# The S5 recurrence of a fp32 decoder layer in chunks of eight tokens

## The chip, the cores and the metric

The kernel runs on one core of a Trainium2 chip. Its engines are named as the profile names them: PE multiplies matrices (PEld loads its weights), DVE and ACT work elementwise, POOL fills and issues some DMAs, SP issues nearly all DMAs. SBUF holds tiles of 128 partitions, PSUM holds what PE writes. The metric is the device time of one execution in microseconds (us). A kernel's time is the median of its runs. Everything is computed in fp32 or in pairs of rounded fp32 halves ("hi" and "lo", type fp32r on PE).

## What is computed

One layer of a hybrid decoder: 512 prompt tokens and 8 sequences of 8 sample tokens (576 columns in all), width 2048. One wide projection of x feeds three mixers (S5, gated linear attention, a convolution), whose gated outputs are merged, projected, normalised. Only S5 concerns the change. It has 64 groups of 16 channels; each group has 64 complex states that decay on their own:

```python
def s5_mixer(u, h0_re, h0_im, a_re, a_im, log_dt, b_re, b_im, c_re, c_im, d):
    lam = lax.complex(a_re, a_im)
    dt = jnp.exp(log_dt)[:, None]
    a_bar = jnp.exp(lam * dt)
    b_bar = ((a_bar - 1.0) / lam)[..., None] * lax.complex(b_re, b_im)
    bu = jnp.einsum('btgc,gpc->btgp', ug, b_bar)
    bu = bu.at[:, 0].add(a_bar * h0)
    _, h = lax.associative_scan(combine, (a_seq, bu), axis=1)   # h[t] = a_bar * h[t-1] + bu[t]
    c = lax.complex(c_re, c_im)
    y = jnp.einsum('btgp,gcp->btgc', h, c).real + d * ug
    return y, h[:, -1].real, h[:, -1].imag
```

The prompt starts from a zero state, each sample sequence from its own given state h0. After it come GELU, a gated product, and a projection. The last states are outputs too.

## The kernel before

**The weight stream.** All dense products are jobs of `run_jobs`. A job makes 128 output channels for all 576 columns from a column block of a weight matrix. Its weights come in units of eight k-tiles (512 KB, line 313, three buffers `raw`), are split by ACT into `hi` (line 70 through `split` and `prep`) and by DVE into `lo` (line 77), and PE makes three products for each k-tile (hi by x hi, hi by x lo, lo by x hi), each in two pieces of 288 columns (line 347). So a k-tile is six products, half a unit 24, a unit 48, and a job with 16 k-tiles 96. Two PSUM accumulators `mm` take turns.

**Background work.** S5, attention and convolution are Python generators. Between two half units the emitter calls `pump`, which gives each running generator a credit worth some microseconds of DVE; a `yield` with a number spends credit, a bare `yield` waits for the next half unit. That fixes the order in which the program is written. A scheduler with a timeline then sets the order of each engine's queue; an instruction whose data it thinks late is moved behind others. Once set, each engine takes its queue in order.

**S5 before.** The jobs of the first part are eight blocks of u (128 channels, eight groups, four pairs of groups), each followed by five gate jobs. For each block `s5_block` splits u, copies the halves to pairs with 16 DMAs (line 596), loads B and C, turns both by 4 transposes, and spreads B with 16 DMAs (line 629). For each of the four pairs, `s5_front` makes B u for the real and imaginary part (4 products of 128x128 weights and 288 columns, fp32r, line 649) and a table of cosines and sines for all 576 columns; `s5_back` rotates, runs the real decay as a scan over all 512 tokens (line 696) and one over the samples (698), and rotates back. `s5_out` multiplies with C: 16 fp32 products on four column tiles of PE (line 726), adds d u, applies GELU and stores a tile `yd`, which `ys_load` reads back much later. Transposes stand under line 99, elementwise DVE operations under 77, 90, 92, 95, ACT under 70: these are helpers.

Of the kernel before, what the change touches and what calls it, by code (L numbers as in the profile page):

```python
# [8 lines left out]
F32 = mybir.dt.float32  # L9
# [31 lines left out]
class K:  # L41
# [9 lines left out]
    # ------------------------------------------------------------ helpers  # L51
# [125 lines left out]
    # ------------------------------------------------------------ constants  # L177
# [27 lines left out]
    def vectors(self):  # L205
        """Channel vectors, one column for each block of 128."""
# [3 lines left out]
        par = c([128, 1], I32, name="par")  # L210
        nc.vector.tensor_scalar(par, part, 4, 1, op0=OP.logical_shift_right, op1=OP.bitwise_and)
        self.par = c([128, 4], F32, name="parf")
        self.ts(self.par[:, 1:2], par, 1.0)
        self.ts(self.par[:, 0:1], par, -1.0, 1.0)
        self.ts(self.par[:, 2:4], self.par[:, 0:2], -1.0)
# [71 lines left out]
    # ------------------------------------------------------------ weight stream  # L287
# [3 lines left out]
    def run_jobs(self):  # L291
# [60 lines left out]
        # the first two jobs advance together, a block of x at a time  # L352
# [69 lines left out]
    # ------------------------------------------------------------ S5  # L422
    def s5_prep(self):
# [93 lines left out]
        # rotation tables, entries 0..63, for all pairs, eight pairs to a slot  # L517
# [5 lines left out]
        def double(m, tc_, ts_, j0, nj):  # L523
            n = 2 ** m
            cm = self.cos[:, m, j0:j0 + nj, None].to_broadcast([128, nj, n])
            sm = self.sin[:, m, j0:j0 + nj, None].to_broadcast([128, nj, n])
# [22 lines left out]
        # sample states: a_bar * h0 as [(g2 p), part, s, pair]  # L549
# [9 lines left out]
        self.ah0 = self.alloc()  # L559
        nc.gpsimd.memset(self.ah0[:, 512:], 1.0)  # L560
        nc.gpsimd.memset(self.ah0[:, 512:].rearrange("p (s e) -> p s e", s=8)[:, :, 0:1], 0.0)
        self.mk64 = self.ah0[:, 512:]
        ah = self.ah0[:, :512].rearrange("p (t s j) -> p t s j", t=2, s=8)
        hv = p.rearrange("p (t s j) -> p t s j", t=2, s=8)
        tm = h0[:, :256].rearrange("p (s j) -> p s j", s=8)
        ar, ai = abr[:, None, :].to_broadcast([128, 8, 32]), abi[:, None, :].to_broadcast([128, 8, 32])
        self.mul(ah[:, 0], hv[:, 0], ar)
        self.mul(tm, hv[:, 1], ai)
        self.sub(ah[:, 0], ah[:, 0], tm)
        self.mul(ah[:, 1], hv[:, 1], ar)  # L570
        self.mul(tm, hv[:, 0], ai)
        self.add(ah[:, 1], ah[:, 1], tm)
        self.free(h0)
        self.ST = self.alloc()
        self.done.add("s5prep")
        yield 2.0

    def s5_block(self, b, st):
        """Block b of four pairs: its operands."""
# [3 lines left out]
        u = self.u[b]  # L583
        uh, ul = self.split(u)
        w, e = self.alloc(), self.alloc()
        st["w", b] = w
        # C of this block, [(g2 p), (g8 c)] with the other group of each pair zero
        for pt, nm in enumerate(("s5_c_re", "s5_c_im")):
            nc.sync.dma_start(e[:, 256 + pt * 64:320 + pt * 64], i[nm][0, 8 * b:8 * b + 8].rearrange("g c p -> (g c) p"))
            for g in range(2):  # L590
                self.pin(self.act(e[:, pt * 128 + g * 64:pt * 128 + g * 64 + 64], e[:, 256 + pt * 64:320 + pt * 64],
                                  scale=self.par[:, 2 * pt + g:2 * pt + g + 1]))
        us = [self.alloc(F32R) for _ in range(4)]
# [3 lines left out]
        self.free(uh, ul)  # L597
        st["us", b] = us
        # B of this block, [(g2 p), pair, (g2' c)] with the other group of each pair zero
        z = self.alloc()  # L600
        nc.gpsimd.memset(z[:, 0:256], 0.0)
        for pt, nm in enumerate(("s5_b_re", "s5_b_im")):
            nc.sync.dma_start(z[:, 256 + 64 * pt:320 + 64 * pt].rearrange("q (j c) -> q j c", j=4),
                              i[nm][0, 8 * b:8 * b + 8].rearrange("(j g) p c -> (g p) j c", g=2))

# [3 lines left out]
        yield  # L609
        for pt, (x, y, op) in enumerate(((256, 320, OP.subtract), (320, 256, OP.add))):  # L610
            self.mul(v(384), v(x), fr)
            self.mul(v(448), v(y), fi)
            zz = z[:, pt * 128:(pt + 1) * 128].rearrange("q (j c) -> q j c", j=4)
            for g in range(2):
                q = slice(g * 64, g * 64 + 64)
                self.tt(zz[q, :, g * 16:g * 16 + 16], v(384)[q], v(448)[q], op)
        p = self.aux()
        for pt in range(2):
            self.tr(p[:, pt * 128:(pt + 1) * 128], z[:, pt * 128:(pt + 1) * 128])
            self.tr(p[:, 256 + pt * 128:384 + pt * 128], e[:, pt * 128:(pt + 1) * 128])  # L620
        yield 1.0
        bt = self.alloc(F32R)
        self.act(bt[:, 0:256], p[:, 0:256])
        self.act(w[:, 0:256], p[:, 256:512])
        self.sub(bt[:, 256:512], p[:, 0:256], bt[:, 0:256].bitcast(F32))
        lb = [self.alloc(F32R) for _ in range(2)]
        for d in range(4):
            for q in range(4):
                nc.sync.dma_start(lb[d // 2].bitcast(F32)[32 * q:32 * q + 32, (d % 2) * 256:(d % 2) * 256 + 256],
                                  bt.bitcast(F32)[32 * d:32 * d + 32, (q // 2) * 256:(q // 2) * 256 + 256])  # L630
        self.free(e, z, bt)
        st["lb", 2 * b], st["lb", 2 * b + 1] = lb
        yield 0.4
        for _ in range(BLK_WAIT):
            yield

    def s5_front(self, j, st):
        """Pair j of groups: B u and its rotation table."""
        nc = self.nc
        b, jj = divmod(j, 4)  # L640
        lb = st["lb", j // 2]
        # B u
        us = st["us", b][jj]
        bu = self.alloc(), self.alloc()
        for pt in range(2):
            o = (jj % 2) * 256 + pt * 128
            for h in range(2):
                p = self.aux()
                nc.tensor.matmul(p[:, :H], lb[:, o:o + 128], us[:, h * H:(h + 1) * H], start=True, stop=True)  # L649
                self.act(bu[pt][:, h * H:(h + 1) * H], p[:, :H])  # L650
            for _ in range(B_WAIT):
                yield
        # e^(i theta t)
        Ct, St, tmp = self.alloc(), self.alloc(), self.alloc()
        g, o = divmod(j, 8)
        for x, y in ((Ct, self.TC[g]), (St, self.TS[g])):
            self.act(x[:, 0:64], y[:, o * 64:(o + 1) * 64])
            self.act(x[:, 512:576].rearrange("p (s e) -> p s e", s=8), y[:, None, o * 64:o * 64 + 8].to_broadcast([128, 8, 8]))
        for m in range(6, 9):
            n = 2 ** m  # L660
            cm, sm = self.cos[:, m, j:j + 1], self.sin[:, m, j:j + 1]
            self.act(tmp[:, 0:n], St[:, 0:n], scale=sm)
            self.act(tmp[:, 256:256 + n], Ct[:, 0:n], scale=sm)
            self.stt(Ct[:, n:2 * n], Ct[:, 0:n], cm, tmp[:, 0:n], OP.mult, OP.subtract)
            self.stt(St[:, n:2 * n], St[:, 0:n], cm, tmp[:, 256:256 + n], OP.mult, OP.add)
            if m == 7:
                yield 0.7
        self.free(tmp)
        yield 0.7
        self.free(us)  # L670
        if jj % 2:
            self.free(lb)
        st["f", j] = (Ct, St, bu)

    def s5_back(self, j, st):
        """Pair j: rotation into the frame in which the decay is real, scan, rotation back."""
        nc = self.nc
# [1053 lines left out]
```

## Time and profile before

| what | value |
|---|---|
| median of 2 runs | 2398.74 us (2397.85 to 2399.63) |
| span of the profiled execution, first to last instruction | 2393.7 us |
| time of the profiled execution apart from its span | not recorded by itself; the median lies 5.0 us above the span |
| mean granted clock of PE over the span | 0.996 |
| S5 beside the stream | from about 60 to about 740 us |
| longest part of the chain by line | L347, 93% |

The page's second part cuts the span into 40 slices of 60 us. Each digit is the busy share of a slice in tenths:

```profile
PE   8999999999999999999999999999999999999998
PEld 7999999999999999999999999999999999999997
DVE  4889989989895443299998875344444553344556
ACT  4444544454445533332222233232232232232332
POOL 0000000000001010000000000000000000000000
PEclk9999999999999999999999999999999999999998
DMA  7444344444433343243333534344443323232223
```

S5 lies in slices 2 to 13, attention behind it up to slice 18, then the convolution. Two things help in reading on. A product's listed mean of some 295 ns is its length in the pipeline; the time from one start to the next is what a product costs PE. And an engine that is busy is not the one that sets the end unless others wait for it, which the chain (part 4 of the page) and the waits say.

### The profile page before, as it was taken

To read this page: it belongs to the slowest core of one execution; us is meant where nothing else is said; L and a number is where in the kernel's file an instruction comes from. 1 tells how busy PE (TensorE), PEld (TensorE's weight loads), DVE (VectorE), ACT (ScalarE), POOL (GpSimd) and SP (SyncE) were. 2 spreads that over 40 slices of the span, in tenths; PEclk is the share of its full clock that TensorE was granted. 3 is DMA by queue.
4 is the path that set the end of the run, shared out by engine and by line. 5 is a ranking of instruction groups with operands and counts; after the bars stand their busy time and mean duration, and the time that the engine had idled before them with its cause. 6 is when DMAs were issued, how large, how long until landed. Compare 5 with 4: busy or idle time off the path is not lost.

```text
span 2393.7 us, 44249 instructions
## 1 busy us (share of the span) xinstructions
PE 2378.1 (99%) x17908; PEld 2339.5 (98%) x17908; DVE 1549.4 (65%) x3084; ACT 861.0 (36%) x1802; POOL 33.3 (1%) x76
## 2 busy tenths in 40 slices
PE   8999999999999999999999999999999999999998
PEld 7999999999999999999999999999999999999997
DVE  4889989989895443299998875344444553344556
ACT  4444544454445533332222233232232232232332
POOL 0000000000001010000000000000000000000000
PEclk9999999999999999999999999999999999999998
DMA  7444344444433343243333534344443323232223
GB/s 204 120 120 133 106 138 128 122 118 124 132 96 91 104 126 111 81 147 108 94 85 105 155 96 144 86 128 118 123 116 112 110 80 88 80 96 82 80 76 101
DMA packets 424605, 267.13 MB, mean 112 GB/s; under 512 B 25673, under 2 KB 395917, under 8 KB 424385
## 3 DMA queue, kind: packets, MB, share of 16 engines
q1 hardware_dynamic: 421904, 256.87, 38.1%
q0 software_dynamic: 2496, 7.43, 0.9%
q8 instruction: 141, 2.31, 0.4%
q14 instruction: 64, 0.52, 0.1%
HBM read 219.22 MB, written 32.07 MB: 105 GB/s over the span
## 4 chain that ended last, share of the span: by engine, by line
PE 98%; DMA 1%; DVE 0%; SPq 0%; ACT 0%; issue 0%; DVEq 0%; ACTq 0%
PE mm L347 93%; PE aux L99 1%; PE two L99 1%; PE aux L649 1%; PE two L726 1%; DVE sl L95 0%; DMA sl<-in_x_sample 0%; PE two L963 0%; PE aux L962 0%; DMA sl<-in_w_in 0%; PE two L965 0%; DMA sl<-in_x_prompt 0%; PE two L1005 0%; PE two L814 0%; PE aux L940 0%; PE two L1001 0%
## 5 line engine op out<-in xcount | busy, mean ns | idle before, releaser
L347 PE MATMUL mm<-xh,hi 128*128 128x288 f32 (+1 forms) x4096 | 886.2, 298 | 2.4 <-ACT hi L70 1.9
L347 PE MATMUL mm<-xl,hi 128*128 128x288 f32 (+1 forms) x4096 | 886.8, 297 | 0.0
L347 PE MATMUL mm<-xh,lo 128*128 128x288 f32 (+1 forms) x4064 | 875.6, 296 | 0.0
L70 ACT ACTIVATE hi<-raw 128x512 fp32r<-128x512 f32 (+1 forms) x696 | 435.3, 626 | 1198.0 <-PE mm L347 1160.4
L77 DVE TENSOR_TENSOR lo<-raw,hi 128x512 fp32r<-128x512 f32 (+1 forms) x692 | 471.1, 681 | 571.4 <-ACT hi L70 534.5
L347 PEld LDWEIGHTS mm<-xh,hi 128*128 128x128 f32 x4096 | 659.1, 189 | 8.9 <-issue 2.8
L347 PEld LDWEIGHTS mm<-xl,hi 128*128 128x128 f32 x4096 | 661.0, 189 | 2.9 <-issue 1.2
L347 PEld LDWEIGHTS mm<-xh,lo 128*128 128x128 f32 x4064 | 655.4, 189 | 1.0 <-issue 0.4
L77 DVE TENSOR_TENSOR sl<-sl,sl 128x576 f32<-128x576 f32 (+9 forms) x842 | 502.8, 625 | 57.0 <-ACT sl L70 48.2
L347 PE MATMUL mm<-sl,hi 128*128 128x288 f32 x2944 | 510.3, 295 | 0.0
L347 PEld LDWEIGHTS mm<-sl,hi 128*128 128x128 f32 x2944 | 432.2, 188 | 0.5 <-ACT sl L70 0.2
L347 PE MATMUL mm<-sl,lo 128*128 128x288 f32 x1472 | 314.3, 295 | 0.0
L347 PEld LDWEIGHTS mm<-sl,lo 128*128 128x128 f32 x1472 | 236.7, 188 | 0.0
L95 DVE SCALAR_TENSOR_TENSOR sl<-sl,cw,sl 128x64 f32<-128x64 f32 (+1 forms) x480 | 216.3, 512 | 0.0
L70 ACT ACTIVATE sl<-sl 128x64 f32<-128x64 f32 (+5 forms) x293 | 107.8, 403 | 95.8 <-DVE sl L77 42.0
L70 ACT ACTIVATE sl<-sl,sl 128x128 f32<-128x128 f32 (+2 forms) x192 | 70.7, 411 | 37.8 <-DVE sl L95 27.3
L77 DVE TENSOR_TENSOR sl<-mm,sl 128x576 f32<-128x576 f32 x48 | 36.3, 756 | 70.9 <-PE mm L347 70.9
L70 ACT ACTIVATE sl<-mm,bias 128x576 f32<-128x576 f32 x112 | 81.2, 725 | 0.1
L696 DVE TENSOR_TENSOR_SCAN sl<-s5r,sl 128x512 f32<-128x512 f32 x64 | 77.9, 1217 | 0.0
L70 ACT ACTIVATE sl<-aux 128x288 f32<-128x288 f32 (+8 forms) x221 | 72.8, 371 | 11.1 <-PE aux L962 3.4
L95 DVE SCALAR_TENSOR_TENSOR sl<-sl,sl,sl 128x128 f32<-128x128 f32 (+2 forms) x192 | 64.3, 365 | 4.4 <-ACT sl L70 4.2
L70 ACT ACTIVATE sl<-two 128x128 f32<-128x128 f32 (+6 forms) x58 | 20.1, 352 | 65.8 <-DVE sl L1451 34.5
(181 smaller groups left out, 800.6 us busy)
## 6 DMA issues: line engine op xcount, KB each, us to landing
raw<-in_w_in SPq DMA_DIRECT2D x223, 512.0 KB
raw<-in_w_o SPq DMA_DIRECT2D x32, 512.0 KB
raw<-in_w_pg SPq DMA_DIRECT2D x32, 512.0 KB
gd<-sl SPq DMA_DIRECT2D x48, 288.0 KB
sl<-gd SPq DMA_DIRECT2D x48, 288.0 KB
sl<-sl SPq DMA_DIRECT2D x128, 72.0 KB
raw<-in_p_gla SPq DMA_DIRECT2D x16, 512.0 KB
raw<-in_p_s SPq DMA_DIRECT2D x16, 512.0 KB
```

What stands on the lines that cost most here:

```text
L70: return self.nc.scalar.activation(out, in_, func, **kw)
L77: self.nc.vector.tensor_tensor(out, a, b, op)
L95: self.nc.vector.scalar_tensor_tensor(out, a, s, b, op0=op0, op1=op1)
L99: self.nc.tensor.transpose(out, in_, self.ident[:n, :n])
L347: nc.tensor.matmul(ps[:, o:o + n], lh[:, k - ka], rh[k][:, c:c + n], start=a, stop=b)
L649: nc.tensor.matmul(p[:, :H], lb[:, o:o + 128], us[:, h * H:(h + 1) * H], start=True, stop=True)
L696: nc.vector.tensor_tensor_scan(v[:, :512], self.r[:, j:j + 1].to_broadcast([128, 512]), v[:, :512], 0.0, op0=OP.mult, op1=OP.add)
L726: nc.tensor.matmul(p[32 * jj:32 * jj + 32, h * 512:h * 512 + H], cd[:, pt * 128 + 32 * jj:pt * 128 + 32 * jj + 32], hs[jj][pt][:, h * H:(h ...
```

## The change

The 512 tokens become 64 chunks of 8, and the eight sample sequences of 8 tokens eight chunks more: 72 chunks. With one group's 16 channels at 8 places in a chunk, one chunk is a column of 128 numbers. Per block of eight groups:

- The job's end stores u to DRAM in chunk order (`s5_store_u`); eight DMAs bring it back with (place, channel) on the partitions and (group, chunk) along the columns.
- `s5_block` builds, from powers 1 to 8 of a_bar (a new table in `s5_prep`), the rows C a^m and the columns a^m B; eight small products (line 689 of the new kernel) make the strip K of the Toeplitz matrix, which has d on its diagonal; it goes to DRAM, and 16 DMAs bring it back shifted, as `L`. Eight transposes turn the a^m B to `G`.
- `s5_scan` makes each chunk's own contribution to the state (line 728, 16 products), rotates it by the angle of eight tokens, scans over the 64 chunks of four pairs at once (256 columns with resets), rotates back. Samples need no scan: their entry state is h0.
- `s5_out` adds the part from the entry state (line 783, 8 products of 144 columns) and the part within the chunk (787, 8 products of 72), applies GELU and stores with eight DMAs; `s5_load_y` reads back with two ACT copies into token order.
- `s5_finals` makes the samples' last states at the end.

All products of S5 are now fp32, none fp32r. The generator `out` holds `front` back to at most one block ahead.

The diff, cut to its core:

```diff
-        for z in range(4):
-            for q, src in enumerate((uh, ul, uh, ul)):
-                nc.sync.dma_start(us[z].bitcast(F32)[q * 32:(q + 1) * 32], src.bitcast(F32)[z * 32:(z + 1) * 32])
...
-        for d in range(4):
-            for q in range(4):
-                nc.sync.dma_start(lb[d // 2].bitcast(F32)[32 * q:32 * q + 32, (d % 2) * 256:(d % 2) * 256 + 256], ...)
...
+    def s5_store_u(self, b, ps):
+        t = self.alloc()
+        tv = t.rearrange("p (s n) -> p s n", s=8)
+        bias = self.bcol(OFF["s5_u"] + b * 128)
+        for o, w, n in ((0, 288, 8), (512, 224, 44), (736, 64, 0)):
+            self.act(tv[:, :, n:n + w // 8], ps[:, o:o + w].rearrange("p (n s) -> p s n", s=8), AF.Identity, bias=bias)
+        self.nc.sync.dma_start(self.ud[b], t)
...
+        # s5_block
+        U = self.alloc()
+        src = self.ud[b].rearrange("(g c) (s n) -> s c g n", g=8, s=8)
+        for q in range(8):
+            nc.sync.dma_start(U[16 * q:16 * q + 16].rearrange("c (g n) -> c g n", g=8), src[7 - q])
...
+        self.mul(o0, cr, ar)
+        self.mul(tv, cn, ai)
+        self.add(o0, o0, tv)
...
+        for pt in range(2):
+            for jj in range(4):
+                nc.tensor.matmul(p[32 * jj:32 * jj + 32, :128], z[:, pt * 128 + 32 * jj:pt * 128 + 32 * jj + 32],
+                                 cl[pt][:, jj * 144:jj * 144 + 128], start=pt == 0, stop=pt == 1, tile_position=(0, 32 * jj))
+        yield 1.8
...
+        nc.sync.dma_start(self.kd[b], kt[:, :256])
...
+        for pt in range(2):
+            p = self.aux()
+            for jj in range(4):
+                self.tr(p[:, jj * 128:(jj + 1) * 128], g[pt][:, jj * 128:(jj + 1) * 128])
+            yield 0.2
+            self.act(G[pt][:, :512], p)
...
+        for q in range(8):
+            for a in range(2):
+                nc.sync.dma_start(L[a][16 * q:16 * q + 16, :512].rearrange("c (g w) -> c g w", g=4),
+                                  src[:, 4 * a:4 * a + 4, 16 + 16 * q:144 + 16 * q])
...
+        # s5_scan
+        for pt in range(2):
+            for gg in range(8):
+                jj, h = divmod(gg, 2)
+                nc.tensor.matmul(X[64 * h:64 * h + 64, pt * 512 + jj * 72:pt * 512 + jj * 72 + 72],
+                                 G[pt][:, gg * 64:gg * 64 + 64], U[:, gg * 72:gg * 72 + 72], start=True, stop=True,
+                                 tile_position=(0, 64 * h))
...
+        for o in (0, 256):
+            nc.vector.tensor_tensor_scan(w[:, o:o + 256], rm[:, :256], w[:, o:o + 256], 0.0, op0=OP.mult, op1=OP.add)
...
-            nc.vector.tensor_tensor_scan(v[:, :512], self.r[:, j:j + 1].to_broadcast([128, 512]), v[:, :512], 0.0,
-                                         op0=OP.mult, op1=OP.add)
...
         # s5_out
         p = self.two()
-        for h in range(2):
+        for jj in range(4):
+            o = (jj // 2) * 512 + (jj % 2) * 144
             for pt in range(2):
-                for jj in range(4):
-                    nc.tensor.matmul(p[32 * jj:32 * jj + 32, h * 512:h * 512 + H],
-                                     cd[:, pt * 128 + 32 * jj:pt * 128 + 32 * jj + 32],
-                                     hs[jj][pt][:, h * H:(h + 1) * H], start=pt == 0, stop=pt == 1,
-                                     tile_position=(0, 32 * jj))
+                nc.tensor.matmul(p[:, o:o + 144], cl[pt][:, jj * 144 + 16:jj * 144 + 144], hs[pt][:, jj * 144:jj * 144 + 144],
+                                 start=pt == 0, stop=False)
+            for h in range(2):
+                gg = 2 * jj + h
+                nc.tensor.matmul(p[:, o + h * 72:o + h * 72 + 72], L[gg // 4][:, (gg % 4) * 128:(gg % 4) * 128 + 128],
+                                 U[:, gg * 72:gg * 72 + 72], start=False, stop=h == 1, skip_group_check=h == 0)
...
-        nc.sync.dma_start(self.yd[0, b], u)
+        dst = self.yd[0, b].rearrange("(g c) (s n) -> s c g n", g=8, s=8)
+        for s in range(8):
+            nc.sync.dma_start(dst[s], u[16 * s:16 * s + 16].rearrange("c (g n) -> c g n", g=8))
```

How the order of the queues moves, at three places. In these rows a name with a number behind it is a tile, `x2` says that a row stands twice, and the sizes are weight columns by moving columns for PE and the shape for SP.

PE before, a block's B u and, half a unit and more later, its output between weight products. B u, one part of one pair:

```order
L347 MATMUL mm<-xh_87,hi 128x288 x2
L347 MATMUL mm<-xl_103,hi 128x288 x2
L347 MATMUL mm<-xh_87,lo 128x288 x2
L649 MATMUL aux<-sl_2108,sl_2217 128x288 x2
L347 MATMUL mm<-xh_88,hi 128x288 x2
```

PE after, the strip K of block 3, in two pieces with eleven weight products between them:

```order
L350 MATMUL mm<-xh_84,hi 128x288 x2
L689 MATMUL aux<-sl_3536,sl_3456 32x128 x4
L350 MATMUL mm<-xl_100,hi 128x288 x2
L350 MATMUL mm<-xh_84,lo 128x288 x2
L350 MATMUL mm<-xh_85,hi 128x288 x2
L350 MATMUL mm<-xl_101,hi 128x288 x2
L350 MATMUL mm<-xh_85,lo 128x288 x2
L350 MATMUL mm<-xh_86,hi 128x288
L689 MATMUL aux<-sl_3537,sl_3456 32x128 x4
```

Before, what S5 gave to PE stood on the borders of half units. After, the scheduler has put the strip (and likewise the transposes behind it and L728) in between, where it reckons their operands ready; the sixteen pieces of B u in a block are gone.

PE before, the start of a block's output, on column tiles (the same eight follow for the second half of the columns):

```order
L347 MATMUL mm<-xh_99,lo 128x288 x2
L726 MATMUL two<-sl_1749,sl_1400 32x288
L726 MATMUL two<-sl_1927,sl_1400 32x288
L726 MATMUL two<-sl_2133,sl_1400 32x288
L726 MATMUL two<-sl_2474,sl_1400 32x288
L726 MATMUL two<-sl_1750,sl_1400 32x288
```

PE after, the start of a block's output, on the whole array (`sl_3646` is a tile of L, `sl_3446` is u in chunk order, `sl_3536` and `sl_3537` are C a^m, `sl_3723` and `sl_3724` the entry states):

```order
L350 MATMUL mm<-xh_91,lo 128x288 x2
L783 MATMUL two<-sl_3723,sl_3536 128x144
L783 MATMUL two<-sl_3724,sl_3537 128x144
L787 MATMUL two<-sl_3446,sl_3646 128x72 x2
L783 MATMUL two<-sl_3723,sl_3536 128x144
```

The output now needs, besides the states, the strip that came back from DRAM.

SP before, around the spreading of B of block 1:

```order
L596 DMA sl_2110<-sl_2096 32x576
L313 DMA raw<-in_w_in 128x8x128 x2
L1193 DMA gd<-sl_2162 128x576
L629 DMA sl_2217<-sl_2213 32x256 x8
L629 DMA sl_2218<-sl_2213 32x256 x8
L313 DMA raw<-in_w_in 128x8x128 x2
```

SP after, block 2: u out and in (`ud`), then the strip out and in (`kd`); of the sixteen loads of L two are shown:

```order
L316 DMA raw<-in_w_in 128x8x128 x3
L600 DMA ud<-sl_2536 128x576
L613 DMA sl_2541<-ud 16x8x72 x8
L316 DMA raw<-in_w_in 128x8x128
L1278 DMA gd<-sl_2731 128x576
L316 DMA raw<-in_w_in 128x8x128
L696 DMA kd<-sl_2637 128x256
L710 DMA sl_2741<-kd 16x4x128
L710 DMA sl_2742<-kd 16x4x128
```

Before, the small DMAs went from SBUF to SBUF. After, each group of loads stands right behind the store that it reads, and a weight load stands behind each group.

More of the change, by code (lines that the diff above doesn't have):

```diff
@@ L516, in s5_prep @@
         self.t32, self.fre, self.fim = t32, fre, fim
+        self.r8 = c([128, 32], F32, name="s5r8")
+        self.act(self.r8, lr, AF.Exp, scale=8.0)
+        self.pw = self.alloc()
+        pr, pi = (self.pw[:, o:o + 256].rearrange("p (m j) -> p m j", m=8) for o in (0, 256))
+        tq = self.alloc()
+        self.act(pr[:, 0], abr)
+        self.act(pi[:, 0], abi)
+        for n in (1, 2, 4):
+            tv = tq[:, :32 * n].rearrange("p (m j) -> p m j", m=n)
+            ar, ai = (x[:, n - 1:n].to_broadcast([128, n, 32]) for x in (pr, pi))
+            br, bi = pr[:, 0:n], pi[:, 0:n]
+            cr, ci = pr[:, n:2 * n], pi[:, n:2 * n]
+            self.mul(cr, br, ar)
+            self.mul(tv, bi, ai)
+            self.sub(cr, cr, tv)
+            self.mul(ci, br, ai)
+            self.mul(tv, bi, ar)
+            self.add(ci, ci, tv)
+        self.free(tq)
+        yield 4.0
         TC, TS, tmp_ = self.alloc(), self.alloc(), self.alloc()
@@ new lines, in s5_block @@
+        yield 1.9
+        self.mul(o1, cn, ar)
+        self.mul(tv, cr, ai)
+        self.sub(o1, o1, tv)
+        yield 1.9
+        g = [e, self.alloc()]
+        gv = [x[:, :512].rearrange("p (j m c) -> p j m c", j=4, m=8) for x in g]
+        bv = [v(256), v(320)]
+        for pt in range(2):
+            self.act(gv[pt][:, :, 0, :], bv[pt])
+        sh = [128, 4, 7, 16]
+        br, bi = (x[:, :, None, :].to_broadcast(sh) for x in bv)
+        ar, ai = (x[:, :, 0:7, None].to_broadcast(sh) for x in (pr, pi))
@@ new lines, in s5_block @@
+        self.free(t, z)
+        G = [self.alloc() for _ in range(2)]
+        for pt in range(2):
+            p = self.aux()
+            for jj in range(4):
+                self.tr(p[:, jj * 128:(jj + 1) * 128], g[pt][:, jj * 128:(jj + 1) * 128])
+            yield 0.2
+            self.act(G[pt][:, :512], p)
+        self.free(*g)
+        L = [self.alloc() for _ in range(2)]
+        src = self.kd[b].rearrange("(g c) w -> c g w", g=8)
+        for q in range(8):
+            for a in range(2):
+                nc.sync.dma_start(L[a][16 * q:16 * q + 16, :512].rearrange("c (g w) -> c g w", g=4),
+                                  src[:, 4 * a:4 * a + 4, 16 + 16 * q:144 + 16 * q])
@@ L714, in s5_out @@
     def s5_out(self, b, st):
         nc = self.nc
-        u = self.u[b]
-        cd = st["w", b]
-        hs = [st.pop(("h", 4 * b + jj)) for jj in range(4)]
+        hs = st.pop(("hs", b))
+        U, cl, G, L = st.pop(("op", b))
         for _ in range(OUT_WAIT):
@@ L776, in s5, with s5_finals @@
             self.spawn(g, "s5")
+    def s5_finals(self):
+        sv = self.ST.rearrange("p (t s j) -> p t s j", t=2, s=9)[:, :, 1:9]
+        h0 = self.h0T[:, :512].rearrange("p (t s j) -> p t s j", t=2, s=8)
+        xs = self.XS[:, :512].rearrange("p (t j s) -> p t s j", t=2, j=32)
+        mr, mi = (self.pw[:, None, o + 224:o + 256].to_broadcast([128, 8, 32]) for o in (0, 256))
+        t = self.alloc()
+        tv = t[:, :256].rearrange("p (s j) -> p s j", s=8)
+        for pt, (x, y, op) in enumerate(((0, 1, OP.subtract), (1, 0, OP.add))):
+            self.mul(sv[:, pt], h0[:, x], mr)
+            self.mul(tv, h0[:, y], mi)
+            self.tt(sv[:, pt], sv[:, pt], tv, op)
+            self.add(sv[:, pt], sv[:, pt], xs[:, pt])
+        self.free(t)
     def s5_states(self):
@@ L1277, in build @@
             c = OFF["s5_u"] + n * 128
[L1278 removed]
+            self.job(w_in, c, X, lambda ps, n=n: self.s5_store_u(n, ps))
             g_jobs(NG_S5)
```

285 lines of the change are left out of this document (139 added, 146 removed).

## The prediction

> **What bounds the kernel now.** I read the page's busy table and its chain first, then the waits of PE, then windows, then the chain in order of time around one S5 block.
>
> ```profile
> span 2393.7 us, 44249 instructions
> ...
> PE 2378.1 (99%) x17908; PEld 2339.5 (98%) x17908; DVE 1549.4 (65%) x3084; ACT 861.0 (36%) x1802; POOL 33.3 (1%) x76
> ...
> PE 98%; DMA 1%; DVE 0%; SPq 0%; ACT 0%; issue 0%; DVEq 0%; ACTq 0%
> ```
> ```profile
> PE two L99 <- DMA sl<-in_x_prompt: 3.4, 1, 3.4
> PE mm L347 <- ACT hi L70: 1.9, 1, 1.9
> PE two L99 <- DVE sl L77: 1.1, 1, 1.1
> ```
> ```profile
> 300.00:400.00 100.00, 100.00 (x768) 98.70 (x768) 90.94 (x183) 44.14 (x114) 0.31 (x1) 1.00 0.49 134
> 1500.00:1600.00 100.00, 100.00 (x752) 100.00 (x751) 35.94 (x51) 28.78 (x46) 0.00 (x0) 1.00 0.36 100
> ```
>
> PE is busy for 2378.1 of 2393.7 us, the chain is PE for 98%, and the largest wait of PE by its releaser is 3.4 us, at the start. All of PE's idle time is 15.6 us. The window rows (columns: PE, PEld, DVE, ACT, POOL busy, then the granted clock, the DMA share and GB/s) are one stretch with S5 beside the weight stream and one without. PE is full in both and its clock is 1.00 in both, though DVE is at 90.94 in one and at 35.94 in the other. So DVE and ACT work of S5 is covered by the weight stream, and taking it away buys nothing by itself. Only what S5 puts on PE's queue, and waits that PE would newly make, can move the end. The median of the runs, 2398.74, lies 5.0 us above this execution's span; I keep these 5.0 us as they are and work with the span.
>
> **What the change takes off PE, per block of four pairs.**
>
> ```profile
> 169.02 0.44 PE aux L99 x4
> ...
> 179.04 0.26 PE aux L649 x2
> ```
> ```profile
> 359.59 3.20 PE mm L347 x24
> 362.79 2.08 PE two L726 x32
> 364.87 3.38 PE mm L347 x24
> 368.24 0.27 PE aux L649 x2
> ```
>
> These are pieces of the chain: start, length, work. 24 weight products take 3.20 us, 0.133 each. A block had 16 products B u (L649): eight pairs at 0.265, 2.12 us. It had 4 transposes at 0.44. Its output (L726), 16 fp32 products on four column tiles, shows as 32 records and 2.08 us, and the 24 weight products behind it take 3.38 and not 3.20, so 0.18 for leaving the column tiles: 2.26. Sum 4.82 us, times 8 blocks 38.6 us.
>
> **What it puts on PE, per block.** No operation of the new shapes is in the trace, so each is bounded by the nearest.
>
> ```profile
> 2198.27 0.55 PE two L99 x5
> ```
> ```profile
> 813.82 0.60 PE L963 MATMUL two<-sl,sl 128*128 128x256 f32 x2
> 814.25 0.59 PE L962 MATMUL aux<-sl,sl 128*128 128x256 f32 x2
> 814.68 0.59 PE L965 MATMUL two<-sl,sl 128*128 128x256 f32 x2
> ```
> ```profile
> 815.27 0.17 PE aux L939 x2
> 815.44 0.22 PE aux L940 x2
> ```
> ```profile
> 828.04 0.24 PE aux L985 x16
> 828.28 0.37 PE aux L99 x2
> ```
>
> - Ten transposes of 128x128 (two of C, eight of the powers of B) at 0.55/5 = 0.11: 1.10 us.
> - Eight fp32 products on the whole array with 144 columns (L783). One fp32 product with 256 columns starts 0.43 us after the one before (813.82, 814.25, 814.68), 1.68 ns for a column: 144 columns are 0.242, eight 1.94 us.
> - Eight fp32 products on the whole array with 72 columns (L787). By columns they would be 0.121 each, 0.97 together. But L939 and L940, fp32 with 64 columns, take 0.17 and 0.22 where their columns make 0.107: below some length the weights set the pace. I take 0.21 each, 1.70 us; ends 0.97 and 1.76.
> - Sixteen fp32 products of 64 weight columns on two column tiles, 72 moving columns (L728). By columns, two at a time, 8 x 0.121 = 0.97 us. If nothing overlapped and each cost as L939 and L940 do, 16 x 0.195 = 3.1 us. The nearest row is L985: 8 fp32 products of 32 weight columns on column tiles, 16 records in 0.24 us, so 0.03 for a product with almost no moving columns. That speaks for the low end; I take 1.2.
> - Eight fp32 products of 32 weight columns on four column tiles, 128 moving columns (L689): L726 scaled by columns and count, 2.08 x 8/16 x 128/288 = 0.46 us. The upper end is 8 x 0.195 = 1.56.
> - Leaving column tiles: L689 and L728 each stand in two pieces between weight products, so 4 x 0.18 = 0.72 us; ends 0.18 and 0.9.
>
> Sum 7.12 us, times 8 is 57.0 us. The lower ends make 5.62 and 45.0, the upper 10.4 and 83. Against the 38.6 taken off, PE has 18.4 us more to do, between 6 and 44.
>
> The pace of loading weights has a rule. The Trainium skill, "TensorE: Matmul & The Clock Gate", section "LDWEIGHTS (loading the stationary operand)", puts it at P/1.2 ns for P weight columns, whatever the depth: an estimate of 107 ns for a pass of 128 columns. L939 and L940 agree, 0.17 and 0.22 us for two passes. By the rule the L728 products, 32 passes of 64 columns one behind the other, would take 1.7 us and not 1.2, and the forecast would be 4 us later. The L985 row disagrees there: 16 passes of 32 columns in 0.24 us, where the rule makes 0.43. I stay with the row.
>
> **What it takes off and puts on the other engines.**
>
> ```profile
> L77 DVE TENSOR_TENSOR lo<-raw,hi 128x512 fp32r<-128x512 f32 (+1 forms) x692 | 471.1, 681 | 571.4 <-ACT hi L70 534.5
> ...
> L696 DVE TENSOR_TENSOR_SCAN sl<-s5r,sl 128x512 f32<-128x512 f32 x64 | 77.9, 1217 | 0.0
> ```
> ```profile
> L77 DVE TENSOR_TENSOR sl<-sl,sl 128x576 f32<-128x576 f32 x398 | 286.3, 749 | 3.7 <-ACT sl L70 2.5 <-DMA gd<-sl 0.5
> ```
>
> DVE: a pair had 12 operations of 576 columns (749 ns) and two long scans (1217 ns), 11.4 us, four times in a block: 46 us, beside small ones (in these rows the number after the bar is the group's busy time, then the mean ns of one). Now a block has 12 operations of 448 or 512 columns, by the 681 ns of the first row at most 8.2 us, 14 of at most 256 columns, at most half of 749 and some overhead each, about 6, and two scans of 256 columns, about half of 1217 each: some 15 us. The three operations of the output stay. Once, the preparation gains 18 small operations for the powers, and the end eight of 256 columns for the sample states. Over eight blocks DVE loses above 200 us. Its cover is the whole weight stream, so this is costed at nothing. If PE had waited for DVE, it would be the gain; the waits of PE show 1.1 us.
>
> ACT empties the u products with three strided copies and not one. The other accumulator is in use for the next job's 96 products, 12.8 us, so this is hidden. The read back of y adds two copies for each of eight tiles, on an engine at 36%. POOL's fills stay on an engine at 1%.
>
> SP: 37 DMAs in a block become 40, of like size. The new thing is that two of them are stores to DRAM that the next ones on SP must wait for: u (then 8 loads) and the Toeplitz strip (then 16 loads). Behind them stand the weight loads.
>
> ```profile
> out<-sl POOLq DMA_DIRECT2D x16, 256.0 KB, 3.0
> ...
> out<-sl POOLq DMA_DIRECT2D x8, 128.0 KB, 2.8
> ...
> out<-sl POOLq DMA_DIRECT2D x2, 16.0 KB, 2.4
> ```
> ```profile
> 239.59 8.32 SPq L313 DMA_DIRECT2D raw<-in_w_in  x2
> 248.31 11.85 SPq L629 DMA_DIRECT2D sl<-sl  x16
> 260.26 0.53 SPq L1193 DMA_DIRECT2D gd<-sl  x1
> 260.88 1.13 SPq L313 DMA_DIRECT2D raw<-in_w_in  x2
> ```
> ```profile
> 186.09 0.63 ACT L70 ACTIVATE hi<-raw 128x512 fp32r<-128x512 f32 x1 [2.54 <-DMA raw<-in_w_in]
> ```
>
> Sixteen small loads hold SP for 11.85 us already today, and 13 us pass between two weight loads (247.9 to 260.88). The worst that follows is ACT waiting 2.54 us for a weight tile, and PE not at all. The wait for the strip adds about 2.8 us to such a gap. I cost this at nothing. Were the cover gone, PE would wait for part of 2.8 us, eight times: at most 22 us.
>
> The tightest new path ends at the output. In the order of PE 131 weight products stand between the second L689 piece and L783, with eight transposes and L728: 17.5 + 0.9 + 1.6 = 20.0 us. In that time go one copy and one small DVE operation (0.6), the store (2.8), sixteen issues (11.85) and the last landing (2.4): 17.7 us. The margin is 2.3 us if SP is free when the strip is ready. For u, 144 products, 19.2 us, stand against 3.0 + 8 x 0.74 + 2.4 = 11.3.
>
> **The rivals.**
>
> - Cheap small products. L787 and L728 run at their column pace and leaving tiles costs little: the lower ends, +6 us, 2405. L985 speaks for it, L939 and L940 against.
> - PE waits for the strip (slower). If SP is late, every output product L787 waits on PE's own queue, with all weight products behind it. Each microsecond past the margin costs 8 us. For 2% (48 us) 30 must come on top of 18.4: 3.7 us a block, so the last strip load 6.0 us later than worked out, say with sixteen issues at 1.1 us each: 18.4 + 30, about 2447. For it speaks the thin margin, against it that today's 32 such loads a block, with like sizes, never held PE. The Trainium skill, "DMA: Bandwidth & Descriptors", section "Specifications", asks for pieces of at least 512 bytes for full rate; the loads of u and the stores of y come in 288-byte pieces, the strip in 512. No row here prices such pieces.
> - The relief of DVE shows on PE. Then the idle 15.6 us would shrink; even if all went, 2417 would become 2401. The S5 part of PE and its idle time together are 54 us, so a gain above 2% would need nearly all of both.
>
> **How the numbers follow.** 2398.7 + 18.4 = 2417 us. The sum as worked out, give or take the ends of single terms (2411 to 2428): chance 0.58. Cheap small products (up to 2411): 0.20. Dear small products or short waits for strip, u or weights (2428 to 2446): 0.13. The strip sets the pace (above 2447): 0.07. Below 2399: 0.02. The range 2404 to 2440 leaves out the last two, part of the dear case and the lowest of the cheap. 2% either way is about what a measurement of this kernel can tell from no change: 2351 to 2447. Faster 0.01, within 0.91, slower 0.08.
>
> **What would show it.** PE still near 99%, chain still PE. In the chain, a block's output should be one piece of about 3.6 us for 32 records, the two L728 pieces about 0.6 each, the L689 pieces about 0.23 each, four transposes 0.44. DVE's busy time down by 200 us or more with no change in PE's pace of 0.133 us. In PE's waits, a line for L787 with a DMA as releaser would show the strip late; a line for mm with ACT hi would show the weight stream late behind SP. I am wrong if S5 pieces of PE sum to less than 45 or more than 83 us, or if PE waits above some 10 us in the S5 stage.

## The result, and the profile after

The kernel after the change takes 2420.69 us (median of 2 runs, 2420.34 to 2421.04) against 2398.74: a ratio of 1.0094, 95% interval 1.0064 to 1.0123. It is 22.0 us slower: under 1%, but the interval is clear of 1. The forecast was 2417.

The page of the kernel after: span, busy time by engine, chain by engine.

```profile
span 2418.6 us, 43944 instructions
```
```profile
PE 2402.9 (99%) x18212; PEld 2366.2 (98%) x18212; DVE 1253.1 (52%) x2480; ACT 784.2 (32%) x1496; POOL 45.6 (2%) x101
```
```profile
PE 99%; DVE 0%; ACT 0%; DMA 0%; SPq 0%; issue 0%; DVEq 0%; ACTq 0%
```

The waits of PE in the kernel after, the largest two (us in total, times, longest), and the S5 window shown before (busy time of PE, PEld, DVE, ACT, POOL, then clock, DMA share, GB/s):

```profile
PE two L99 <- DMA sl<-in_x_prompt: 3.3, 1, 3.3
PE mm L350 <- ACT hi L70: 2.0, 1, 2.0
```
```profile
300.00:400.00 100.00, 100.00 (x815) 97.58 (x814) 42.62 (x83) 32.68 (x72) 3.05 (x7) 1.00 0.44 115
```

DVE lost 296 us (1549.4 to 1253.1), in the S5 window more than half of its load (90.94 to 42.62). PE was full before and is full now, and its idle time (span less busy time) is 15.7 us where it was 15.6. No wait for S5's transfers is among PE's waits. What changed the time is PE's own work, and the chain in order of time shows it piece by piece. This is one block (start, length, work; L350 is the weight product):

```profile
296.36 0.22 PE aux L99 x2
296.57 6.66 PE mm L350 x50
303.24 0.36 PE aux L689 x8
303.59 1.65 PE mm L350 x11
305.24 0.35 PE aux L689 x8
305.59 1.92 PE mm L350 x13
307.52 0.44 PE aux L99 x4
307.95 1.58 PE mm L350 x12
309.54 0.44 PE aux L99 x4
309.97 1.32 PE mm L350 x10
311.30 0.65 PE two L728 x16
311.95 0.59 PE mm L350 x3
312.54 0.65 PE two L728 x16
313.19 12.58 PE mm L350 x93
325.77 0.49 PE two L783 x4
326.26 0.40 PE two L787 x4
...
329.47 5.63 PE mm L350 x42
```

The S5 pieces add up to 1.10 (ten transposes) + 0.71 (L689) + 1.30 (L728) + 3.70 (L783 and L787, from 325.77 to 329.47) = 6.81 us. Behind each of the four column-tiled pieces the weight products are too long by some 0.18: 11 at 0.1333 would be 1.47 and take 1.65, 3 would be 0.40 and take 0.59. That is another 0.73, in all 7.54. As a cross-check, take the time from the first L783 of one block to that of the next, and subtract its weight products. In after that is 84.34 us with 576 weight products; before, from one L726 to the next (362.79 in the prediction), it is 78.41 us with 552:

```profile
410.11 0.49 PE two L783 x4
```
```profile
284.38 2.08 PE two L726 x32
```

At 0.1334 us a weight product some 7.5 us are left over in after and 4.8 before (7.51 and 4.79 with the pace unrounded); below, this remainder is called a block's left-over. 8 x (7.51 - 4.79) = 21.8 us, against 22.0 measured. Nothing is left for waits.

The strip's transfers on SP for the same block (start, length, issue; `kd` holds the strip in DRAM):

```profile
306.66 0.33 SPq L696 DMA_DIRECT2D kd<-sl  x1
309.36 8.45 SPq L710 DMA_DIRECT2D sl<-kd  x16
```

The store of the strip is waited for (2.7 us from 306.66 to 309.36), the sixteen loads take 8.45 us to issue, and they are out at 317.81. The first output product, L783, starts at 325.77, 8.0 us later; L783 does not read the strip, and L787, which does, starts at 326.26, 8.45 us later.

### The profile page after: what moved, and what is told of

Same layout as the page of the kernel before. It is cut to its first block, busy times and chain, and to the rows that moved or that the text cites. A ratio compares the mean times of both kernels' runs of the same rounds, so it can differ in the third digit from the quotient of the medians.

```text
span 2418.6 us, 43944 instructions
## 1 busy us (share of the span) xinstructions
PE 2402.9 (99%) x18212; PEld 2366.2 (98%) x18212; DVE 1253.1 (52%) x2480; ACT 784.2 (32%) x1496; POOL 45.6 (2%) x101
## 4 chain that ended last, share of the span: by engine, by line
PE 99%; DVE 0%; ACT 0%; DMA 0%; SPq 0%; issue 0%; DVEq 0%; ACTq 0%
PE mm L350 93%; PE aux L99 1%; PE two L99 1%; PE two L783 1%; PE two L787 1%; PE two L728 0%; DVE sl L95 0%; PE two L1048 0%; PE aux L1047 0%; PE aux L689 0%; PE two L1050 0%; PE two L1090 0%; PE two L899 0%; PE aux L1025 0%; PE two L1086 0%; DMA sl<-in_w_in 0%
## 5 line engine op out<-in xcount | busy, mean ns | idle before, releaser
L350 PE MATMUL mm<-xh,hi 128*128 128x288 f32 (+1 forms) x4096 | 889.6, 298 | 2.4 <-ACT hi L70 2.0
L350 PE MATMUL mm<-xl,hi 128*128 128x288 f32 (+1 forms) x4096 | 890.3, 297 | 0.0
L350 PE MATMUL mm<-xh,lo 128*128 128x288 f32 (+1 forms) x4064 | 876.2, 296 | 0.0
L350 PEld LDWEIGHTS mm<-xh,hi 128*128 128x128 f32 x4096 | 659.9, 189 | 7.0 <-ACT hi L70 2.1
L350 PEld LDWEIGHTS mm<-xl,hi 128*128 128x128 f32 x4096 | 660.9, 189 | 4.6 <-issue 3.0
L350 PEld LDWEIGHTS mm<-xh,lo 128*128 128x128 f32 x4064 | 655.8, 189 | 1.0 <-issue 0.4
L350 PE MATMUL mm<-sl,hi 128*128 128x288 f32 x2944 | 511.5, 296 | 0.0
L350 PEld LDWEIGHTS mm<-sl,hi 128*128 128x128 f32 x2944 | 433.3, 189 | 0.3
L77 DVE TENSOR_TENSOR sl<-sl,sl 128x576 f32<-128x576 f32 (+10 forms) x542 | 296.8, 573 | 79.8 <-ACT sl L70 51.9
L350 PE MATMUL mm<-sl,lo 128*128 128x288 f32 x1472 | 314.9, 296 | 0.0
L350 PEld LDWEIGHTS mm<-sl,lo 128*128 128x128 f32 x1472 | 237.2, 189 | 0.0
L70 ACT ACTIVATE sl<-sl 128x576 fp32r<-128x576 f32 (+10 forms) x247 | 104.1, 442 | 96.1 <-DVE sl L77 47.2
L70 ACT ACTIVATE sl<-mm,bias 128x576 f32<-128x576 f32 (+3 forms) x128 | 83.7, 667 | 0.3
L70 ACT ACTIVATE sl<-two 128x128 f32<-128x128 f32 (+6 forms) x90 | 31.9, 376 | 96.8 <-DVE sl L1537 34.4
L70 ACT ACTIVATE sl<-aux 128x256 fp32r<-128x256 f32 (+7 forms) x134 | 42.3, 331 | 37.7 <-PE aux L99 13.5
L99 PE MATMUL aux<-ident,sl 128*128 128x128 f32 (+5 forms) x248 | 44.2, 274 | 0.0
L99 PEld LDWEIGHTS aux<-ident,sl 128*128 128x128 f32 (+5 forms) x248 | 31.8, 142 | 2.3 <-issue 1.7
L99 PE MATMUL two<-ident,sl 128*128 128x128 f32 (+2 forms) x175 | 28.3, 281 | 4.6 <-DMA sl<-in_x_prompt 3.3
```

The costliest lines, as they stand in the source:

```text
L70: return self.nc.scalar.activation(out, in_, func, **kw)
L77: self.nc.vector.tensor_tensor(out, a, b, op)
L99: self.nc.tensor.transpose(out, in_, self.ident[:n, :n])
L350: nc.tensor.matmul(ps[:, o:o + n], lh[:, k - ka], rh[k][:, c:c + n], start=a, stop=b)
```

## The experiments

All results are medians of device time; each ratio is to runs of the kernel before on the same chip (medians 2398.37 to 2398.79 there). After was not run again beside them, so a difference of some tenths of a us to its 2420.69 says nothing. The theory is that only PE's own work moved the end. Its rivals are that DVE's relief paid back a part, that transfers cost something, and that the products' price is other than the chain makes it look.

**1. DVE's load put back.** In the generator `back`, behind the scan:

```diff
+                x = self.alloc()
+                for _ in range(12):
+                    for _ in range(4):
+                        self.mul(x, self.h0T, self.h0T)
+                    yield 3.0
+                self.free(x)
```

> The kernel after the change, with 48 extra multiplications of 128x576 into a scratch tile in every block (about 36 us of DVE a block, 290 us in all), spread over the time right behind the scan; results unchanged. It puts DVE's load back to about that before the change and leaves TensorE's work alone. Theory (only TensorE's own work counts): 2420.7 plus or minus 3 us, DVE up by about 290 us to some 1540. Rival (the relief of DVE had paid back part of the added TensorE work): 5 to 15 us longer than after, with new waits of TensorE for DVE or ACT.

Measured: 2426.48 us, 1.0115 (1.0101 to 1.0129), 5.8 us above after. By its time this is the rival. But the waits of PE name one place:

```profile
PE aux L99 <- ACT sl L70: 5.3, 1, 5.3
```

A window of the same kernel shows where (columns as above):

```profile
800.00:900.00 100.00, 94.24 (x685) 89.28 (x685) 48.02 (x98) 58.73 (x117) 3.46 (x5) 0.97 0.33 94
```

In the S5 window, 300 to 400 us, DVE is at 77.75 and PE stays full. The loss stands behind S5, where the attention heads are prepared: the added `yield 3.0` spent credit, so the S5 generators ended later (the last L783 starts at 761.7, in after at 666.0, and before the change the last output product at 738.0). Attention's preparation began late, and PE waited for it once. The run measured a delay as well as a load, so it does not decide. The granted clock in the window shown, in which PE waits, is 0.97; in the S5 window it is 1.00.

**2. DVE's load taken from the kernel before.** Of the rotations of every pair only two multiplications stay; for the first rotation:

```diff
         self.mul(vr, Ct, br)
-        self.mul(tmp, St, bi)
-        self.add(vr, vr, tmp)
         yield 2.0
-        self.mul(vi, Ct, bi)
-        self.mul(tmp, St, br)
-        self.sub(vi, vi, tmp)
+        self.mul(vi, St, bi)
```

> The kernel before the change, with 10 of the 12 rotation operations of every pair taken out on DVE (about 240 us); it leaves out the rotations of the S5 states, so the S5 part computes something else. TensorE's work is unchanged. Theory (DVE is covered by the weight stream): the same as before, 2398.7 plus or minus 3 us, TensorE's idle time still about 15 us. Rival (DVE's relief is worth something by itself): 5 to 15 us faster, out of TensorE's idle time.

Measured: 2398.83 us, 0.9999 (0.9990 to 1.0008). DVE fell by 191 us, to 1358.5, and the time stayed. The S5 window:

```profile
300.00:400.00 100.00, 100.00 (x769) 98.70 (x768) 54.35 (x118) 45.16 (x117) 0.31 (x1) 1.00 0.47 124
```

DVE is at 54.35 where it was at 90.94, and PE starts 769 products where it started 768. The relief is worth nothing by itself.

**3. DVE's load put back, without delay.** A fourth generator beside S5's three (`WIDTH` makes room for it):

```diff
+        def pad():
+            while "s5prep" not in self.done:
+                yield
+            while st["back"] < 8:
+                x = self.alloc()
+                for _ in range(2):
+                    self.mul(x, self.h0T, self.h0T)
+                self.free(x)
+                yield
```

> The kernel after the change, with two extra multiplications of 128x576 into a scratch tile at each step of the background work while S5 runs (about 48 a block, some 290 us of DVE in all), put beside S5's own steps and not between them, so that S5 does not end later as it did in the first run with extra multiplications; outputs unchanged. Theory (DVE's load in the S5 stage costs nothing; the 5.3 us that TensorE waited once in that first run came from the GLA preparation being pushed late): within 3 us of after, 2420.7, no wait of TensorE in the GLA preparation above 1 us. Rival (DVE's load itself costs some 6 us): 2425 to 2428.

Measured: 2420.17 us, 1.0094 (1.0078 to 1.0111), the time of after. DVE came up by 170 us, less than meant, to 1423.5; in its S5 window:

```profile
300.00:400.00 100.00, 100.00 (x815) 97.57 (x814) 75.58 (x131) 32.96 (x72) 1.89 (x5) 1.00 0.43 115
```

DVE at 75.58 or at 42.62, PE makes the same 815 products in the same 100 us. With run 2 this settles it for the loads tried: DVE's load in this stage costs nothing, and the 5.8 us of run 1 were its delay.

**4. S5's products twice.** The loops over parts and pairs run twice, as `for pt in (0, 1, 0, 1)` around L689, `(0, 0, 1, 1)` around L728, `for jj in (0, 1, 2, 3, 0, 1, 2, 3)` around L783 and L787, and likewise for the transposes.

> The kernel after the change, with every product and transpose that the change's S5 block issues on TensorE done twice, in the same stretches: ten transposes, 8 products L689, 16 products L728, 8 products with 144 and 8 with 72 columns (L783, L787). Outputs unchanged, and no stretch between column tiles and weight products is added. Theory (TensorE's queue sets the end, each piece costs what its row shows): 1.10 + 0.45 + 0.97 + 3.70 = 6.2 to 6.8 us a block more, 48 to 54 us in all, about 2469 to 2475. Rival A (idle places in the stream absorb part): less than 40 us more. Rival B (the longer pieces make buffers and loads late, so waits come on top): more than 65 us more, with TensorE's waits in the S5 stage.

Measured: 2467.62 us (2465.13 to 2471.3), 1.0285 (1.0270 to 1.0301), 46.9 us above after; a block's left-over is 13.43 against 7.51 us, 8 x 5.92 = 47.4. Part of a block in its chain:

```profile
322.63 0.35 PE aux L689 x8
...
324.64 0.79 PE aux L689 x24
...
332.00 2.15 PE two L728 x64
```

It is 1.4 us below the expected range for a plain reason: the two L728 pieces became one here. The 64 records take 2.15 us where 1.30 + 0.97 was expected at the least, and one leaving of column tiles (0.18) fell away: 0.30 us a block, 2.4 in all. No slack took anything up, and the only new waits of PE are 1.0 us in all. Work of S5 on PE shows in the end one for one.

**5. Fewer column-tiled pieces.** Two bare yields ahead of the L689 products, one more ahead of the scan:

```diff
+        yield
+        yield
         p = self.aux()
...
-                for _ in range(BLK_WAIT):
+                for _ in range(BLK_WAIT + 1):
```

> The kernel after the change, with three more pauses in the S5 generators, so that the two pieces of the L689 products (state columns, four column tiles) become one piece straight ahead of the transposes, and the two pieces of the L728 products (two column tiles) become one. The same products are done, in fewer groups: two stretches of column-tiled products a block and not four. Theory (a stretch of column-tiled products costs a fixed 0.31 us, 0.13 on entering it and 0.18 in the weight product behind it): 0.62 us a block less, 5 us in all, about 2415.7; the joined L728 piece takes 1.1 to 1.2 us and not 1.30, the joined L689 piece 0.55 to 0.6 and not 0.71. Rival (the price goes by product and not by group): the same time as after, within 1 us, joined pieces as long as the two apart.

Measured: 2413.64 us, 1.0062 (1.0050 to 1.0075), 7.05 us below after. The chain of one block (L690, L729, L784 and L788 are L689, L728, L783 and L787):

```profile
304.78 0.57 PE aux L690 x16
305.36 0.59 PE aux L99 x4
...
308.89 6.89 PE mm L350 x53
315.78 1.15 PE two L729 x32
316.93 12.98 PE mm L350 x96
```

Sixteen records in one piece take 0.57, in two 0.71; 32 records in one piece 1.15, in two 1.30. So each piece has a fixed cost of about 0.14 to 0.15 beside its products. Run 4 puts a third point on each line: for L689, 8, 16 and 24 records take 0.35, 0.57 and 0.79; for L728, 16, 32 and 64 records take 0.65, 1.15 and 2.15. What follows it is still too long: 96 weight products 12.98 against 12.81, and the four transposes behind L690 0.59 against 0.44. With two pieces instead of four, 0.29 and two times 0.18 make 0.65 a block. The block's left-over fell by 0.86, to 6.65; most of the rest is in the 53 products, which run at 0.130 and not 0.1334 each (in run 9 the same 53 take 7.11 us). So the fixed cost of a piece is shown, about 0.3 us with what lies behind it, and makes the expected 5 of the 7 us; the other 2 were not expected, and are for the most part the quicker pace told of in the last section.

**6. Half the columns in L787.** `U[:, gg * 72:gg * 72 + 36]` for `+ 72`.

> The kernel after the change, with the products of the Toeplitz weights (L787) over 36 moving columns instead of 72; it leaves out the within-chunk part of half of the columns. Theory (the weights set the pace of these short products): an L787 piece of two products stays at 0.40 us in the chain, the time within 1 us of after, 2420.7. Rival (the columns set the pace): a piece falls from 0.40 to about 0.2 to 0.28, 0.06 to 0.1 for a product, 64 products in all, 4 to 6.5 us less.

Measured: 2420.66 us, 1.0095 (1.0078 to 1.0112), nothing changed. In the chain:

```profile
326.84 0.37 PE two L787 x4
327.21 0.57 PE two L783 x4
```

A pair of pieces is 0.94 as before (0.40 + 0.54). Moving columns are not what a product this short is paid for. What it is paid for is the pass: one record, with one loading of weights; a fp32 product leaves two. The Trainium skill, "TensorE: Matmul & The Clock Gate", section "LDWEIGHTS (loading the stationary operand)", puts the loading of P weight columns at P/1.2 ns, an estimate of 107 ns for 128. L787 is near it: two products of two passes in 0.40, so 0.10 a pass. L728 is not: 32 passes of 64 columns take 1.15 us in run 5, 36 ns each, where the rule makes 53 and half of L787's pass would be 50. So on column tiles passes overlap, or are cheaper by weight column; the runs do not tell these apart. That the price of a whole-array pass goes with its weight columns, and is not the same for every pass, is not shown: no run tried fewer weight columns there.

**7. The strip's loads twice.** `for q in (*range(8), *range(8)):` around the sixteen loads.

> The kernel after the change, with each of the sixteen loads of the Toeplitz strip issued twice into the same place, outputs unchanged. SP's issues for the strip grow from 8.45 to about 17 us a block; the order that the program is given puts L787 about 15 weight products (2.0 us) further back. In after, the output products start 8.0 us behind the last issue, some 5.5 us behind the landing if that takes 2.4. Theory (margin of about 5.5 us, not the 2.3 that the prediction worked out): 8.5 of new issues against 5.5 + 2.0, so TensorE waits about 1 us a block for the strip, up to 8 us in all, with a line of L787 or L783 behind a DMA in its waits. Rival A (margin 2.3 as predicted): about 4 us a block, 30 us or more. Rival B (a late SP first delays the weight loads): waits of mm behind ACT hi in TensorE's waits, also at other places than the output.

Measured: 2419.58 us, 1.0091 (1.0074 to 1.0108), no slower than after. PE does not wait for the strip at all. SP, and the start of the block's output in the chain:

```profile
309.49 15.72 SPq L710 DMA_DIRECT2D sl<-kd  x32
```
```profile
326.75 1.97 PE mm L350 x15
328.72 0.40 PE two L787 x4
```

The loads are out at 325.21, 7.4 us later than in after, and the first L787 starts 3.5 us behind. The scheduler had put 15 weight products between L783 and L787, which cost nothing. The expected wait of 1 us a block did not come, for the terms were off: the new issues took 7.3 us and not 8.5, and in after it is L787, 8.45 us behind the last issue, that needs the strip, and not L783 at 8.0. So the margin of 8.45 us could shrink to 3.5 without a wait; the point at which the strip decides was not reached. A third round of loads was not tried.

**8. Output products in one pass.** On top of run 5, the operands go through one rounding copy each (POOL also fills the unused columns of L):

```diff
+    def rounded(self, x):
+        t = self.alloc(F32R)
+        self.act(t, x)
+        self.free(x)
+        return t
...
+        U = self.rounded(U)
+        cl = [self.rounded(x) for x in cl]
+        hs = [self.rounded(x) for x in hs]
+        L = [self.rounded(x) for x in L]
```

> The joined kernel (one piece of L689 products, one of L728 products a block), with the operands of the output products (L783 and L787) rounded to fp32r by ACT beforehand, seven copies of 128x512 or 128x576 a block, so that each product is one pass and not two; it leaves out the lower bits of these operands. Theory (the output's 3.70 us a block is passes of 128 weight columns at about 0.1 us each, or columns at 0.46 ns as in the weight products): 0.8 to 1.75 us a block for the output, 2 to 2.9 us a block less than the joined kernel, 16 to 23 us in all: 2391 to 2398, at or a little below the kernel before. The new copies are covered (ACT was at 32%). Rival (a fixed cost per product or the copies come late, ACT waits for the strip ahead of its weight-stream copies): less than 10 us gained on the joined kernel's 2413.6, with waits of mm for ACT.

Measured: 2398.37 us, 1.0000 (0.9990 to 1.0009), 15.3 us below the joined kernel and just under the expected gain of 16 to 23. The output in its chain (L797 and L801 are L783 and L787):

```profile
323.67 0.18 PE two L797 x2
...
325.38 44.87 PE mm L356 x336
```

The next block's output starts at 405.19:

```profile
405.19 0.18 PE two L797 x2
```

The sixteen products take 1.71 us (323.67 to 325.38) and not 3.70; a block's left-over is 4.69. Sixteen passes, 0.107 each on average: half the passes, a little under half the time. Joined pieces and single passes together give back all that the change had added to PE (4.79 before), and the time is that of the kernel before.

**9. One pass for the transposes too.** On top of run 8, the transposes of the powers become products of rounded tiles with a rounded unit matrix.

> The kernel of the previous run (joined pieces, output operands rounded to fp32r), and the eight transposes of the powers of B done as fp32r products with a rounded unit matrix, their input rounded by two more ACT copies a block; it leaves out the lower bits of these powers too. Theory (TensorE's passes count, nothing else): a transpose of 128 columns is two passes at about 0.11 us and one pass at 0.055 to 0.06, so 0.4 us a block and 3 to 3.5 us in all less than the previous run's 2398.4, about 2395, just under the kernel before. Rival (the transposes are held by something other than passes, or the added copies come late): no change, 2398 to 2400.

Measured: 2399.69 us (2393.54 to 2401.79), 1.0001 (0.9992 to 1.0009): no gain. In the chain four of them (L714) take 0.39 and not 0.44, and the six products between the column tiles and them take 0.99, 0.19 more than 6 x 0.1334:

```profile
299.89 0.99 PE mm L358 x6
300.88 0.39 PE aux L714 x4
```

The expectation rested on a wrong reading. A fp32 product leaves two records, so L689's eight products are sixteen; a transpose leaves one. By its records it was a single pass of 128 weight columns, 0.109 us, all along, and there was nothing to halve. The little that the transposes gained was lost in the weight products: the 53 ahead of L728, at 6.89 in run 8, take 7.11 here.

## Why the prediction was right

**The bound and the covers.** Held. DVE lost 296 us ("above 200") and gave nothing, as runs 2 and 3 show. ACT and POOL stayed far from full, and no wait of PE for S5's transfers appeared. Run 4 shows the other half of the argument, that PE's S5 work counts one for one.

**What leaves PE.** 4.82 us a block were worked out, 4.79 are left over in the trace.

**What comes to PE.** 7.12 us were worked out; 7.51 are left over, and the pieces add up to 7.54:

| per block | predicted | measured |
|---|---|---|
| ten transposes | 1.10 | 1.10 |
| L783 and L787 | 1.94 + 1.70 | 3.70 (2.11 + 1.60) |
| L728 | 1.20 | 1.30 |
| L689 | 0.46 | 0.71 |
| leaving column tiles | 0.72 | 0.73 |

The term that was mis-sized is L689, "L726 scaled by columns and count": 0.25 too little. L726 stood in one piece for 16 products, so scaling it by count also scaled down what a piece costs however short it is; and L689 stands in two pieces. Run 5 shows that fixed part, about 0.14 a piece. Kept out of the scaling, it makes the term come out: (2.08 - 0.14) x 8/16 x 128/288 = 0.43, and two pieces at 0.14 on top, 0.71 as measured. L728, taken from the near end of its bounds for a row with almost no columns, misses 0.10. Together these are 0.35 of the 0.39 missing, 3 us in all, most of the distance from 2417 to 2420.7. The choice of the L985 row over the two-pass rows for L728 was right: 1.30, near 1.2 and far from 3.1. That it came so near is in part luck. The sum had no fixed part for a piece; measured, the products of L728 are 1.00 (32 records at 0.031), close to the 0.97 of its lower end, and the two pieces add 0.30. By the same measure, more than half of L985's 0.24 us for 16 records would be the fixed part and not a price by product, which no run separated there.

**The price of short products.** L787 at 0.21 each, the end set by the weights, held: 0.20. Runs 6 and 8 show that it is paid by the pass and not by moving columns. L783, costed by its columns at 0.242 each, took 0.26; with L787 a little cheaper, the two misses cancel in part (3.70 against 3.64). Columns did not set its pace alone either: in one pass, run 8, it takes 0.12 us, where 144 columns at the weight products' 0.46 ns would be 0.07.

**The rivals.** Cheap small products fell: L787 takes 0.20 and not the 0.121 of its columns, and leaving tiles costs 0.18. The strip was never late. The margin had been put at 2.3 us with the sixteen issues at 11.85; they take 8.45, so that by the landing of 2.4 taken there some 6.0 us are left to the first L787. That was a mis-sized term in the safe direction: loads from DRAM into 16 partitions issue in 0.53 each, where the loads between SBUF tiles had 0.74. The relief of DVE on PE fell in runs 2 and 3. Neither the short waits of the dear case nor the strip as the limit came.

**The base.** The 5.0 us between span and median were not work around the span. In the recorded runs of before, times lie 1.7 to 3.0 us above their spans; the traced execution was itself 2 to 3 us short, for the reason told in the last part. Since the sum was made of differences, this did not reach the forecast. One remark of the prediction was too cautious: 2% is not what a measurement of this kernel can tell. The interval of the result is 0.3% either way, and 22 us stand clear of it.

## What to carry to other kernels

Where one engine is full from end to end, price a change by what it puts in that engine's queue alone: 296 us less on DVE were worth nothing (runs 2 and 3 tried 191 and 170 of them), 2.7 us more on PE in each of eight blocks were worth 22. Price short whole-array products by their passes (here 0.10 to 0.13 us each, with 128 weight columns and 72 or 144 moving ones). Column-tiled products went by their moving columns: with 32 weight columns on four tiles a record costs 0.061 us at 288 columns (L726, with 0.14 taken off) and 0.027 at 128 (L689). Add a fixed cost for each place at which they interrupt whole-array products. When putting load back as a control, see that it does not also move the end of a stage, or the control measures the move.

## What the runs showed of the hardware

**Column tiles cost about 0.3 us for each interruption**, 0.14 within the piece and 0.18 in the weight products behind it, whatever the number of products in it (runs 4 and 5: 8 to 24 records of L689, 16 to 64 of L728). Whole-array pieces show no such cost: 2, 4 and 8 transposes take 0.22, 0.44 and 0.87, and the 50 weight products behind two of them 6.66, 0.133 each.

**The same weight products run at one of two paces.** Windows of 100 us at 1700, with no S5 in them, for the kernel before as traced, for that of run 2, which differs from it in S5 on DVE only, and for run 8:

```profile
1700.00:1800.00 100.00, 100.00 (x772) 100.00 (x771) 39.16 (x58) 26.85 (x43) 0.00 (x0) 1.00 0.43 123
```
```profile
1700.00:1800.00 100.00, 100.00 (x752) 100.00 (x751) 38.38 (x55) 25.62 (x41) 0.00 (x0) 1.00 0.44 123
```
```profile
1700.00:1800.00 100.00, 100.00 (x771) 100.00 (x770) 39.95 (x57) 27.02 (x44) 0.00 (x0) 1.00 0.44 124
```

772 and 771 products against 752, 0.130 us each against 0.133, with PE full and the clock 1.00 in all three. In both quick traces the stretch runs from about 1640 to 1840 us. The traced execution of run 8 took 2394.1 us, 4.3 less than that run's median. Most executions are not so quick: of 45 runs of the kernel before beside the experiments, of which no trace was kept, two took 2394.4 and 2394.5 us and the others 2397.0 to 2400.8. That these two had the quick stretch is likely and not shown. The same pace stands in runs 5 and 8 in the 53 products of each block. So a single trace can lie 4 us off the median with no change in the kernel: the spans of the traces of before and after differ by 24.9 us, their runs by 22.0. What sets the pace was not found.
